# Down-projection operands split in two parts during gate/up, sample rows' product inside gate/up, and another order of the block products

## The chip, the cores and the metric

The kernel runs on one core of one Trainium2 chip. A core has TensorE (PE, with its weight loads listed as PEld), VectorE (DVE), ScalarE (ACT), GpSimd (POOL) and SyncE (SP), which here issues the DMAs. The metric is the device time of one execution in microseconds (us). Shown is the median of three runs.

## The reference, cut to what matters

One decoder layer in float32 for 1024 prompt rows and 64 sample rows (8 sequences of 8), model width 1024. A mixer (attention and a gated unit) comes first; the change lies in the feed-forward part behind it:

```python
D_FF = 2816
def _ffn(h, w_gate, w_up, w_down):
    return (jax.nn.silu(h @ w_gate) * (h @ w_up)) @ w_down
def _post(x, f, gate, g, b):
    return _layer_norm(ALPHA * x + gate * f, g, b)
...
yp = _post(yp, _ffn(_modulate(yp, mp[3], mp[4]), w_gate[l], w_up[l], w_down[l]),
           mp[5], ln2_g[l], ln2_b[l])
```

## The kernel before

**Two parts for each number.** A float32 product is made of three passes in the float32r type: an operand is split in a rounded part hi (a copy on ACT, `split`, L949) and a rest lo = x - hi (a subtraction on DVE, L950), and hi*hi, lo*hi and hi*lo are summed in PSUM (`PASSES`, L955). `load_unit` (L93) loads 512 KB of weights and splits them so.

**Gate/up.** `gate_up` (L860) runs over the 22 units f of 128 rows of D_FF. For each of three column groups c of X (384, 384 and 320 tokens; the last has 256 prompt tokens and the 64 sample tokens) it makes 24 matmuls into a bank of tag "a" for gate and 24 into one of tag "b" for up, then silu on ACT (L872), the multiplication on DVE (L873), and a store into the DRAM tensor `g_d` (L874). Units 0 and 1 run in the order of `CORD` = (2, 0, 1), half of each ahead of the other half, while the last rows of the mixer are still being made (`norm_tile` L818, `to_features` L163: transposes into banks of tag "c"). Units 2 to 21 stand in the loop at L911.

**The down-projection as seven block products.** The product g @ w_down is cut into 2 x 2 blocks (rows of w_down: two halves of 11 units, j = 0 to 10; columns: halves H[0] and H[1]; prompt tokens: two halves). Seven block products replace eight, in the manner of Winograd's form of Strassen's scheme, so sums of blocks are needed. `down_sums` (L899), called in the loop for f = 2 to 12, loads two rows of w_down, makes four sums on DVE and stores them unsplit into `t_d`. Behind gate/up each product runs over j, loads its two operands, adds and splits them on DVE and ACT, and calls `product` (L957): 12 matmuls of 512 columns, three passes for each of four 128-token blocks, into four PSUM banks (`setA`, `setB`). The first loop (L1033) also computes the 64 sample rows (L1054): 88 matmuls with hi and lo of the sample's g side by side as stationary operand, into two banks `sacc`. Then P2 (L1062), P3 (L1079), P4 (L1097), P5 (L1110), P6 (L1121) and the last (L1161). In P6's loop the operands of the last product are prepared, and the last product runs tile by tile.

**The end of a tile.** `residual` (L1017) multiplies by the gate on POOL and adds ALPHA * x1, loaded from `x1_d`. `close_tile` (L1145) takes statistics, multiplies the finished bank by the gate and adds it. `finish` (L984) makes mean and variance, takes the power -0.5 on POOL (L994), normalises on ACT, multiplies by t_lg on POOL (L101), adds t_lb on DVE (L1008) and stores; the very last tile does this on DVE in halves (L996).

**What sets the order.** The kernel is written in program order; the framework (L1290, `schedule_with_timeline_sim=True`) fixes beforehand the order of the instructions of each engine and of the DMA queue on SP, from a simulated time line and with program order as priority, so work is moved forward where its buffers and inputs are free. On the chip each engine follows that order. Buffers come from pools (`raws`/`rw` two each for raw loads, `wts` four and `w2` two for operands); a pool opened where another was closed shares its memory and waits for it.

Of the kernel before, what the change touches and what calls it, by code (L numbers as in the profile page):

```python
# [10 lines left out]
F32 = mybir.dt.float32  # L11
# [32 lines left out]
def tile_block(  # L44
# [23 lines left out]
    t_d = dram.tile([DFF // 2, 4, 512], F32, name="t_d")  # L68
# [685 lines left out]
    with ExitStack() as p3:  # L754
# [104 lines left out]

        def gate_up(f, ws, cs):  # L860
            for c in cs:
                n = CW[c]
# [11 lines left out]
                nc.sync.dma_start(out=g_d[f * P : (f + 1) * P, 384 * c : 384 * c + n], in_=s[:, :n])  # L874
# [8 lines left out]
    with ExitStack() as p4:  # L883
        rw = p4.enter_context(tc.tile_pool(name="rw", bufs=2, side="right", reuse_waits="tile"))
        g1 = p4.enter_context(tc.tile_pool(name="g1", bufs=2 * NJ, side="right", reuse_waits="tile"))
        gp = p4.enter_context(tc.tile_pool(name="gp", bufs=3, side="right", reuse_waits="tile"))
        oa = p4.enter_context(tc.tile_pool(name="oa", bufs=2, side="right", reuse_waits="tile"))
        tl = p4.enter_context(tc.tile_pool(name="tl", bufs=1, side="right", reuse_waits="tile"))
        tp_ctx = ExitStack()
        tp = tp_ctx.enter_context(tc.tile_pool(name="tp", bufs=1, side="right", reuse_waits="tile"))  # L890

        H = (slice(0, 512), slice(512, D))

# [5 lines left out]
        def down_sums(j):  # L899
            r = tp.tile([P, 2, D], F32, tag="r", name="tpr")  # L900
            for u in range(2):
                nc.sync.dma_start(out=r[:, u], in_=w_down[(j + NJ * u) * P : (j + NJ * u + 1) * P, :])
            b11, b12, b21, b22 = r[:, 0, H[0]], r[:, 0, H[1]], r[:, 1, H[0]], r[:, 1, H[1]]
            t = tp.tile([P, 4, 512], F32, tag="t", name="tpt")
            nc.vector.tensor_tensor(out=t[:, 0], in0=b12, in1=b11, op=ALU.subtract)
            nc.vector.tensor_tensor(out=t[:, 2], in0=b22, in1=b12, op=ALU.subtract)
            nc.vector.tensor_tensor(out=t[:, 1], in0=t[:, 2], in1=b11, op=ALU.add)
            nc.vector.tensor_tensor(out=t[:, 3], in0=b21, in1=t[:, 1], op=ALU.subtract)
            nc.sync.dma_start(out=t_d[j * P : (j + 1) * P], in_=t)

        for f in range(2, NF):  # L911
            gate_up(f, gate_up_open(f), range(3))
            if f < 2 + NJ:
                down_sums(f - 2)
            if f == 2 + NJ:
                tp_ctx.close()
                w2 = p4.enter_context(tc.tile_pool(name="w2", bufs=2, side="right", reuse_waits="tile"))
        x_ctx.close()
        g2 = p4.enter_context(tc.tile_pool(name="g2", bufs=2 * NJ, reuse_waits="tile"))
# [28 lines left out]
        def split(w, cols, src):  # L948
            nc.scalar.activation(out=w[:, 0, cols], in_=src, func=AF.Copy)  # L949
            nc.vector.tensor_tensor(out=w[:, 1, cols], in0=src, in1=w[:, 0, cols].bitcast(F32), op=ALU.subtract)  # L950

        def vtt(out, in0, in1, op):
            nc.vector.tensor_tensor(out=out, in0=in0, in1=in1, op=op)  # L953
# [3 lines left out]
        def product(banks, st, mv, first, last, tbs=range(4)):  # L957
            for tb in tbs:
                for q, (sp, wp) in enumerate(PASSES):
                    mm(out=banks[tb], lhsT=st[sp][:, tb * P : (tb + 1) * P], rhs=mv[wp],  # L960
                       start=first and q == 0, stop=last and q == 2, skip_group_check=True)
# [22 lines left out]
        def finish(i, bns, last=False):  # L984
# [3 lines left out]
            bn = bns  # L988
# [7 lines left out]
            if last:  # L996
                for hs in H:
                    nc.vector.scalar_tensor_tensor(  # L998
                        out=yi[:, hs], in0=yi[:, hs], scalar=mv[:rows, 0:1], in1=lg[:, hs], op0=ALU.subtract, op1=ALU.mult
                    )  # L1000
                    nc.vector.scalar_tensor_tensor(  # L1001
                        out=yi[:, hs], in0=yi[:, hs], scalar=rstd[:rows, 0:1], in1=lb[:, hs], op0=ALU.mult, op1=ALU.add
                    )
                    nc.sync.dma_start(out=dst[:, hs], in_=yi[:, hs])
            else:
                normalize_act(yi, yi, mv, rstd, rows)
                pool_tt(yi, yi, lg, ALU.mult)
                vtt(yi, yi, lb, ALU.add)  # L1008
                nc.sync.dma_start(out=dst, in_=yi)

        def stats_half(bn, i, hf):
# [282 lines left out]
```

## Time and profile before

| what | us |
|---|---|
| median of three runs (lowest, highest) | 1244.11 (1240.84, 1245.77) |
| time of the profiled execution | 1243.76 |
| its span, first to last instruction | 1241.9 |
| PE busy in the span | 1174.6 |
| DVE busy | 636.6 |
| ACT busy | 424.9 |
| POOL busy | 230.2 |

The span is what the trace shows; the time has 1.86 us around it. Busy PE includes matmuls whose ends are modelled, so progress is better read from the starts of successive matmuls. In a timeline a row has its start, its length, engine, line, operation and tiles; in brackets stands how long the engine was idle before it and what released it.

### The profile page before, as it was taken

What the parts mean: (1) busy time and instruction counts of PE and PEld (TensorE: products, weight loads), DVE (VectorE), ACT (ScalarE), POOL (GpSimd) and SP (SyncE); (2) the same over time, 40 slices, a digit from 0 to 9 for tenths busy, and PEclk for the clock granted to TensorE, in tenths of its full rate; (3) what the DMA queues carried; (4) which work ended last, traced back from release to release, by engine and by line L of the source; (5) the groups of instructions that cost most, each with busy time, mean ns of one, the idle gap of its engine ahead of it and who ended that gap; (6) DMA issues with size and microseconds to landing.
All of it is one profiled execution on the core that took longest, in us unless ns stands there. A gap on an engine that the chain in (4) does not pass through costs nothing. (4 is left out here: it accounts for less than half of the span.)

```text
span 1241.9 us, 17503 instructions
## 1 busy us (share of the span) xinstructions
PE 1174.6 (95%) x6791; PEld 1043.8 (84%) x6791; DVE 636.6 (51%) x1212; ACT 424.9 (34%) x749; POOL 230.2 (19%) x202
## 2 busy tenths in 40 slices
PE   4999989999889998999999999999999999999992
PEld 2677678887678798999999999999999977888882
DVE  4444355997757975443121112112113359996886
ACT  3563125666742553211111111111112254444612
POOL 2213434554234430000000000000000003012207
PEclk9999999998999998999999999999999999999997
DMA  9844443322363437777122142112113493433643
GB/s 326 273 136 149 133 151 107 94 83 77 102 237 111 155 134 268 271 258 266 61 93 83 68 160 95 62 60 94 59 59 114 160 330 110 128 110 120 208 148 135
DMA packets 82259, 179.74 MB, mean 145 GB/s; under 512 B 12016, under 2 KB 37744, under 8 KB 80752
## 3 DMA queue, kind: packets, MB, share of 16 engines
q1 hardware_dynamic: 82176, 178.62, 42.6%
q8 instruction: 53, 0.87, 0.3%
q14 instruction: 30, 0.25, 0.1%
HBM read 142.02 MB, written 37.55 MB: 145 GB/s over the span
## 5 line engine op out<-in xcount | busy, mean ns | idle before, releaser
L868 PE MATMUL ps_a<-X,unit 128*128 128x384 f32 (+1 forms) x1584 | 278.2, 328 | 0.6 <-DVE unit L97 0.6
L868 PE MATMUL ps_b<-X,unit 128*128 128x384 f32 (+1 forms) x1584 | 276.0, 326 | 0.0
L868 PEld LDWEIGHTS ps_a<-X,unit 128*128 128x128 f32 x1584 | 263.7, 188 | 1.0 <-DVE unit L97 1.0
L868 PEld LDWEIGHTS ps_b<-X,unit 128*128 128x128 f32 x1584 | 263.3, 188 | 0.0
L873 DVE TENSOR_TENSOR s<-ps_b,s 128x384 f32<-128x384 f32 (+1 forms) x66 | 35.2, 534 | 239.0 <-PE ps_b L868 224.5
L872 ACT ACTIVATE s<-ps_a 128x384 f32<-128x384 f32 (+1 forms) x66 | 31.0, 472 | 358.4 <-PE ps_a L868 353.3
L101 POOL TENSOR_TENSOR y<-y,t_gate 128x512 f32<-128x512 f32 x12 | 18.7, 1584 | 613.4 <-ACT y L1057 555.4
L204 PE MATMUL ps_a<-unit,X 128*128 128x512 f32 x456 | 124.7, 412 | 4.5 <-ACT unit L96 2.4
L97 DVE TENSOR_TENSOR unit<-raw,unit 128x1024 fp32r<-128x1024 f32 x63 | 79.1, 1258 | 94.4 <-ACT unit L96 94.4
L204 PEld LDWEIGHTS ps_a<-unit,X 128*128 128x128 f32 x456 | 86.5, 196 | 33.0 <-issue 5.2
L96 ACT ACTIVATE unit<-raw 128x1024 fp32r<-128x1024 f32 x66 | 69.5, 1057 | 79.5 <-issue 39.3
L488 PE MATMUL ps_a<-X,unit 128*128 128x384 f32 (+1 forms) x408 | 78.4, 340 | 6.0 <-ACT z L498 3.3
L953 DVE TENSOR_TENSOR opnd<-rwd,opnd 128x1024 fp32r<-128x1024 f32 x55 | 68.6, 1258 | 20.2 <-ACT opnd L1048 18.4
L488 PEld LDWEIGHTS ps_a<-X,unit 128*128 128x128 f32 x408 | 69.8, 194 | 7.0 <-ACT z L498 3.5
L204 PE MATMUL ps_b<-unit,X 128*128 128x512 f32 x168 | 49.9, 408 | 0.9 <-DVE X L188 0.9
L960 PE MATMUL ps_d<-opnd 128*128 128x512 f32 x198 | 50.5, 391 | 0.1
L960 PE MATMUL ps_c<-opnd 128*128 128x512 f32 x198 | 50.3, 390 | 0.0
L113 POOL TENSOR_TENSOR rstd<-ve,neghalf 128x1 f32<-128x1 f32 (+1 forms) x36 | 29.8, 827 | 109.0 <-DVE ve L111 93.6
L960 PEld LDWEIGHTS ps_d<-opnd 128*128 128x128 f32 x198 | 37.1, 188 | 8.2 <-DVE y L953 0.5
L960 PEld LDWEIGHTS ps_c<-opnd 128*128 128x128 f32 x198 | 37.2, 188 | 8.1 <-DVE y L953 0.2
L172 ACT ACTIVATE h<-ps_c,mod 128x384 f32<-128x384 f32 (+1 forms) x48 | 29.2, 630 | 42.8 <-PE ps_c L169 29.5
L204 PEld LDWEIGHTS ps_b<-unit,X 128*128 128x128 f32 x168 | 32.2, 195 | 9.3 <-DVE X L188 1.3
(279 smaller groups left out, 1668.0 us busy)
## 6 DMA issues: line engine op xcount, KB each, us to landing
rwd<-in_w_down SPq DMA_DIRECT2D x22, 512.0 KB
raw<-in_w_gate SPq DMA_DIRECT2D x22, 512.0 KB
raw<-in_w_up SPq DMA_DIRECT2D x22, 512.0 KB
tpr<-in_w_down SPq DMA_DIRECT2D x22, 512.0 KB
t_d<-tpt SPq DMA_DIRECT2D x11, 1024.0 KB
g<-g_d SPq DMA_DIRECT2D x44, 256.0 KB
rwd<-t_d SPq DMA_DIRECT2D x44, 256.0 KB
g_d<-s SPq DMA_DIRECT2D x44, 192.0 KB
```

Source lines behind the costliest of these rows:

```text
L96: nc.scalar.activation(out=w[:, 0, :], in_=r, func=AF.Copy)
L97: (lo or nc.vector).tensor_tensor(out=w[:, 1, :], in0=r, in1=w[:, 0, :].bitcast(F32), op=ALU.subtract)
L101: nc.gpsimd.tensor_tensor(out=out, in0=in0, in1=in1, op=op)
L113: nc.gpsimd.tensor_tensor(out=rstd[:rows], in0=ve[:rows], in1=neghalf[:rows], op=ALU.pow)
L172: nc.scalar.activation(out=h[:, :npr], in_=pt[:, :npr], func=AF.Identity, scale=scale_of(mod, k)[:, 0:1], bias=shift_of(mod, k)[:, 0:1])
L204: mm(out=pt, lhsT=X[c][:, xp, k, off : off + P], rhs=rhs_of(units, k, wp), start=st and q == 0, stop=sp and q == 2)
L488: mm(out=pt[:, :n], lhsT=w[:, wp, k * P : (k + 1) * P], rhs=X[c][:, xp, k, :], start=(k == 0 and q == 0), stop=(k == KD - 1 and q == 2))
L868: mm(out=pt[:, :n], lhsT=w[:, wp, k * P : (k + 1) * P], rhs=X[c][:, xp, k, :], start=(k == 0 and q == 0), stop=(k == KD - 1 and q == 2))
L872: nc.scalar.activation(out=s[:, :n], in_=pp[0][:, :n], func=AF.Silu)
L873: nc.vector.tensor_tensor(out=s[:, :n], in0=pp[1][:, :n], in1=s[:, :n], op=ALU.mult)
L953: nc.vector.tensor_tensor(out=out, in0=in0, in1=in1, op=op)
L960: mm(out=banks[tb], lhsT=st[sp][:, tb * P : (tb + 1) * P], rhs=mv[wp], start=first and q == 0, stop=last and q == 2, skip_group_check=True)
```

## The change

Gate/up, besides its old work, now makes the operands of the down-projection in two parts, and the sample rows' product:

- `gate_up` stores only the prompt columns of g. The 64 sample columns are split at once into `gs` and kept in the dictionary `GS`.
- `down_row(f)` replaces `down_sums`. For every unit f it loads row f of w_down, splits it on ACT and DVE and makes the four matmuls of the sample rows into `sacc` (tags "c" and "d"). For f of 11 and more (j = f - 11) it also stores the split half H[1] of that row, loads row j, makes the four sums, stores the first unsplit into `t1_d`, splits the other three and stores both parts of each into `t_d`, which now has room for four operands in two parts. Its pool `tp` lies on the left side and is closed behind gate/up.
- Units 2 to 21 run in the order of `CORD`.
- Four of the products (third, fifth, sixth, seventh) load their moving operand in two parts straight into the operand buffer (`moving`), without ACT or DVE; the first, second and fourth load it unsplit and split it (`moving_split`).
- The order becomes: A11 B11; A12 B21 (last before), in banks of its own; then the third to seventh as below. The last product is the one with A22, and it runs tile by tile over its accumulating banks.
- The gate multiplication of `residual`, the normalisation and the multiplication by t_lg move from POOL and ACT to DVE in all tiles; statistics are taken as halves are finished (`add_and_stats`). Tiles 0 to 3 are finished ahead of the last product, tiles 4 to 7 behind it.

```diff
-                nc.sync.dma_start(out=g_d[f * P : (f + 1) * P, 384 * c : 384 * c + n], in_=s[:, :n])
+                nc.sync.dma_start(out=g_d[f * P : (f + 1) * P, 384 * c : 384 * c + npr], in_=s[:, :npr])
+                if n > npr:
+                    gs = f0.tile([P, 2, NS], F32R, tag="gs", name=f"gs{f}", bufs=3)
+                    nc.scalar.activation(out=gs[:, 0], in_=s[:, npr:n], func=AF.Copy)
+                    nc.vector.tensor_tensor(
+                        out=gs[:, 1], in0=s[:, npr:n], in1=gs[:, 0].bitcast(F32), op=ALU.subtract
+                    )
+                    GS[f] = gs
...
+        sacc = [bank("c"), bank("d")]
+
+        def row_split(src):
+            o = tp.tile([P, 2, D], F32R, tag="o", name="tpo", bufs=2)
+            nc.scalar.activation(out=o[:, 0], in_=src, func=AF.Copy)
+            vtt(o[:, 1], src, o[:, 0].bitcast(F32), ALU.subtract)
+            return o
+
+        def down_row(f):
+            j = f - NJ
+            r = tp.tile([P, D], F32, tag="r", name="tpr", bufs=2)
+            nc.sync.dma_start(out=r, in_=w_down[f * P : (f + 1) * P, :])
+            o = row_split(r)
+            for hf in range(2):
+                for wp in range(2):
+                    mm(out=sacc[hf], lhsT=GS[f].rearrange("p a b -> p (a b)"), rhs=o[:, wp, H[hf]],
+                       start=f == 0 and wp == 0, stop=f == NF - 1 and wp == 1)
+            if j < 0:
+                return
+            rows = slice(j * P, (j + 1) * P)
+            nc.sync.dma_start(out=t_d[rows, 0], in_=o[:, :, H[1]].bitcast(F32))
+            r0 = tp.tile([P, D], F32, tag="r", name="tpr0", bufs=2)
+            nc.sync.dma_start(out=r0, in_=w_down[rows, :])
+            t = tp.tile([P, 4, 512], F32, tag="t", name="tpt")
+            vtt(t[:, 0], r0[:, H[1]], r0[:, H[0]], ALU.subtract)
+            vtt(t[:, 2], r[:, H[1]], r0[:, H[1]], ALU.subtract)
+            vtt(t[:, 1], t[:, 2], r0[:, H[0]], ALU.add)
+            vtt(t[:, 3], r[:, H[0]], t[:, 1], ALU.subtract)
+            nc.sync.dma_start(out=t1_d[rows, :], in_=t[:, 0])
+            o = row_split(t[:, 1:3].rearrange("p a b -> p (a b)"))
             for u in range(2):
...
+                nc.sync.dma_start(out=t_d[rows, 1 + u], in_=o[:, :, H[u]].bitcast(F32))
+            o = tp.tile([P, 2, D], F32R, tag="o", name="tpo", bufs=2)
+            nc.scalar.activation(out=o[:, 0, H[0]], in_=t[:, 3], func=AF.Copy)
+            vtt(o[:, 1, H[0]], t[:, 3], o[:, 0, H[0]].bitcast(F32), ALU.subtract)
+            nc.sync.dma_start(out=t_d[rows, 3], in_=o[:, :, H[0]].bitcast(F32))
 
         for f in range(2, NF):
-            gate_up(f, gate_up_open(f), range(3))
-            if f < 2 + NJ:
-                down_sums(f - 2)
...
+            gate_up(f, gate_up_open(f), CORD)
+            if f == 2:
+                down_row(0)
+                down_row(1)
+            down_row(f)
+        tp_ctx.close()
+        w2 = right("w2", 2)
...
+        def moving(src):
+            w = operand()
+            nc.sync.dma_start(out=w[:, :, H[1]].bitcast(F32), in_=src)
+            return w
+
+        def moving_split(src):
+            w = operand()
+            r = raw()
+            nc.sync.dma_start(out=r[:, 0:512], in_=src)
+            split(w, H[1], r[:, 0:512])
+            return w
...
+        setA = [bank(t) for t in "abcd"]
...
+            A11.append(g_half(g1, j, 0))
+            w = moving_split(w_down[j * P : (j + 1) * P, H[0]])
+            split(w, H[0], A11[j])
+            product(setA, *pair(w), j == 0, j == NJ - 1)
...
+        setB = [bank(t) for t in "abcd"]
         for j in range(NJ):
...
+            w = moving_split(t1_d[j * P : (j + 1) * P, :])
+            t = oa.tile([P, 512], F32, tag="ot", name="ot")
+            nc.sync.dma_start(out=t, in_=g_d[j * P : (j + 1) * P, 512:1024])
+            vtt(t, t, A22[j], ALU.add)
+            split(w, H[0], t)
+            product(setB, *pair(w), j == 0, j == NJ - 1)
+        for tb in range(4):
+            add_and_stats(tb, 0)
+        for tb in range(4):
+            nc.scalar.activation(out=y[:, 4 + tb, H[1]], in_=setB[tb], func=AF.Copy)
...
         for j in range(NJ):
-            w = operand()
-            r = t_half(j, 2)
+            w = moving(t_part(j, 2))
             split(w, H[0], A21[j])
-            split(w, H[1], r[:, H[1]])
             product(setA, *pair(w), False, j == NJ - 1)
+            o = [g1.tile([P, 512], F32R, tag="g", name="ah")]
+            o += [g2.tile([P, 512], F32R, tag="g", name=n_) for n_ in ("al", "bh", "bl")]
+            nc.scalar.activation(out=o[0], in_=A22[j], func=AF.Copy)
+            vtt(o[1], A22[j], o[0].bitcast(F32), ALU.subtract)
+            for lo in range(2):
+                nc.sync.dma_start(out=o[2 + lo].bitcast(F32), in_=t_part(j, 3)[:, lo])
+            ops.append(o)
+        for tb in range(4):
+            add_and_stats(tb, 1)
+            finish(tb, bns[tb])
...
         for tb in range(4):
             vtt(y[:, 4 + tb, H[1]], setA[tb], y[:, 4 + tb, H[1]], ALU.add)
...
         for tb in range(4):
-            close_tile(4 + tb, setA[tb])
...
+            i = 4 + tb
             for j in range(NJ):
                 ah, al, bh, bl = ops[j]
                 for q, (sp, wp) in enumerate(PASSES):
...
+                    mm(out=setA[tb], lhsT=(ah, al)[sp][:, tb * P : (tb + 1) * P], rhs=(bh, bl)[wp],
+                       start=False, stop=j == NJ - 1 and q == 2, skip_group_check=True)
+        for tb in range(4):
+            add_and_stats(4 + tb, 1)
+        for tb in range(4):
+            i = 4 + tb
+            t = oa.tile([P, 512], F32, tag="ot", name="ot")
+            vtt(t, setA[tb], tails["gate"][:, H[0]], ALU.mult)
+            nc.vector.scalar_tensor_tensor(
+                out=y[:, i, H[0]], in0=y[:, i, H[0]], scalar=ALPHA, in1=t, op0=ALU.mult, op1=ALU.add
+            )
+            stats_half(bns[i], i, 0)
+            finish(i, bns[i], tb == 3)
```

More of the change, by code (lines that the diff above doesn't have):

```diff
@@ L1011, in stats_half @@
-        def stats_half(bn, i, hf):
-            rows = rows_of(i)
-            nc.vector.bn_stats(out=bn[:rows, hf, :], in_=y[:rows, i, H[hf]])
-        x1t = {}
-        def residual(i, hf, acc=None):
-            rows = rows_of(i)
-            if i not in x1t:
-                x1t[i] = raw()
-                nc.sync.dma_start(out=x1t[i][:rows], in_=x1_d[i * P : i * P + rows, :])
+            for hs in H if last else (slice(0, D),):
+                nc.vector.scalar_tensor_tensor(
+                    out=yi[:, hs], in0=yi[:, hs], scalar=mv[:rows, 0:1], in1=lg[:, hs], op0=ALU.subtract, op1=ALU.mult
+                )
+                nc.vector.scalar_tensor_tensor(
+                    out=yi[:, hs], in0=yi[:, hs], scalar=rstd[:rows, 0:1], in1=lb[:, hs], op0=ALU.mult, op1=ALU.add
+                )
+                nc.sync.dma_start(out=dst[:, hs], in_=yi[:, hs])
@@ L1075, in tile_block @@
         for tb in range(4):
+            nc.scalar.activation(out=y[:, tb, H[0]], in_=setA[tb], func=AF.Copy)
+        setC = [bank(t) for t in "abcd"]
+        for j in range(NJ):
+            A12.append(g_half(g2, j + NJ, 0))
+            w = moving_split(w_down[(j + NJ) * P : (j + NJ + 1) * P, H[0]])
+            split(w, H[0], A12[j])
+            product(setC, *pair(w), j == 0, j == NJ - 1)
+        for hf in range(2):
+            add_and_stats(8, hf)
+        finish(8, bns[8])
+        for tb in range(4):
+            vtt(y[:, tb, H[0]], setC[tb], y[:, tb, H[0]], ALU.add)
@@ L1079, in tile_block @@
         for j in range(NJ):
-            w = operand()
-            t = t_half(j, 1)
-            vtt(A21[j], A11[j], A21[j], ALU.subtract)
-            vtt(t[:, H[0]], A22[j], A21[j], ALU.subtract)
-            nc.scalar.activation(out=w[:, 0, :], in_=t, func=AF.Copy)
-            vtt(w[:, 1, :], t, w[:, 0, :].bitcast(F32), ALU.subtract)
-            product(setA, *pair(w), False, j == NJ - 1)
-        for hf in range(2):
-            residual(8, hf)
-        bn8 = small.tile([P, 2, 6], F32, tag="bn", name="bn8")
@@ L1105, in tile_block @@
+            t = oa.tile([P, 512], F32, tag="ot", name="ot")
+            vtt(t, A12[j], A22[j], ALU.subtract)
+            vtt(t, t, A21[j], ALU.add)
+            split(w, H[0], t)
             product(setB, *pair(w), False, j == NJ - 1)
@@ L1159, in tile_block @@
         for tb in range(4):
-            close_tile(4 + tb, setA[tb])
-        for tb in range(4):
-            acc = bank("aabb"[tb])
+            i = 4 + tb
             for j in range(NJ):
```

197 lines of the change are left out of this document (52 added, 145 removed).

## The prediction

> **What bounds the kernel now.** I read the page first, then busy time by stretch, then TensorE's (PE's) rows in order of time, then the end. P1 to P7 are the seven block products in program order.
>
> ```profile
> span 1241.9 us, 17503 instructions
> PE 1174.6 (95%) x6791; PEld 1043.8 (84%) x6791; DVE 636.6 (51%) x1212; ACT 424.9 (34%) x749; POOL 230.2 (19%) x202
> ```
>
> ```profile
> 447.70:585.00 137.30, 132.77 (x800) 131.41 (x798) 73.93 (x121) 41.16 (x65) 11.33 (x9) 0.98 0.72 254
> 585.00:700.00 115.00, 115.00 (x702) 115.00 (x701) 20.28 (x25) 16.64 (x24) 0.00 (x0) 1.00 0.27 91
> ...
> 980.00:1035.00 55.00, 53.12 (x234) 42.86 (x232) 34.41 (x44) 28.30 (x41) 2.96 (x3) 1.00 0.82 286
> 1035.00:1066.00 31.00, 30.05 (x123) 24.06 (x124) 30.85 (x35) 14.66 (x15) 6.92 (x4) 0.94 0.36 109
> ...
> 1220.00:1242.00 22.00, 0.00 (x0) 0.00 (x0) 15.94 (x23) 3.72 (x3) 13.23 (x7) 0.61 0.36 143
> ```
>
> The columns are the stretch, its length, busy time of PE, PEld, DVE, ACT and POOL, granted clock, DMA share and GB/s. Gate/up has PE full (115.00 of 115.00) with DVE and ACT four fifths idle. The products are nearly full too, and the last 22 us have no matmul at all.
>
> ```profile
> 531.53 4.35 PE L868 MATMUL ps_a<-X,unit 128*128 128x384 f32 x24
> ...
> 555.23 4.35 PE L868 MATMUL ps_a<-X,unit 128*128 128x384 f32 x24
> ```
>
> ```profile
> 981.83 1.55 PE L960 MATMUL ps_c<-opnd,oa 128*128 128x512 f32 x6
> ...
> 1035.53 0.73 PE L960 MATMUL ps_a<-opnd 128*128 128x512 f32 x2 [2.12 <-ACT opnd L1068]
> ...
> 1036.92 1.84 PE L960 MATMUL ps_a<-opnd 128*128 128x512 f32 x4 [0.20 <-DVE opnd L953]
> ...
> 1172.95 1.53 PE L960 MATMUL ps_c<-opnd 128*128 128x512 f32 x6
> ...
> 1175.68 1.52 PE L960 MATMUL ps_c<-opnd 128*128 128x512 f32 x6
> ...
> 1204.16 15.57 PE L1166 MATMUL ps_b<-o,o 128*128 128x512 f32 x66
> ```
>
> One unit f of gate/up takes 555.23 - 531.53 = 23.70 us for 144 matmuls, without gaps. Twelve 512-column matmuls, one step j of a product, take 1175.68 - 1172.95 = 2.73 us: 0.2275 us each. From 981.83 to the end of the last matmul (1204.16 + 15.57 = 1219.73) are 237.9 us for 7 x 132 + 88 = 1012 matmuls, which need 230.2. So only **7.7 us** of that stage is lost, most of it at 1033 to 1040: a gap of 2.12 us, then four matmuls in 1.84 us instead of 0.91. [...]
>
> **The end.** Rows in order of time:
>
> ```profile
> 1220.55 0.68 DVE L953 TENSOR_TENSOR tt<-ps_b,t_gate 128x512 f32<-128x512 f32 x1
> ...
> 1227.02 5.29 POOL L101 TENSOR_TENSOR y<-y,t_lg 128x1024 f32<-128x1024 f32 x2
> ...
> 1230.05 3.35 DVE L953 TENSOR_TENSOR y<-y,t_lb 128x1024 f32<-128x1024 f32 x1 [1.52 <-POOL y L101]
> 1233.31 0.68 DVE L953 TENSOR_TENSOR y<-y,tt 128x512 f32<-128x512 f32 x1
> 1234.03 0.69 DVE L1013 BATCH_NORM_STATS2 bn<-y 128x6 f32<-128x512 f32 x1
> 1234.63 1.21 DVE L953 TENSOR_TENSOR y<-y,t_lb 128x1024 f32<-128x1024 f32 x1
> ...
> 1238.16 0.99 SPq L1004 DMA_DIRECT2D out<-y  x2
> ```
>
> The last tile is not slow by its own work: its 'y<-y,tt' at 1233.31 stands in DVE's queue behind two 't_lb' additions, which wait for POOL's multiplications by t_lg; one takes 3.35 us beside POOL, the next 1.21.
>
> **The change, part by part.** Base: this execution, span 1241.9, time 1243.76 (1.86 us around the span), 0.35 us under the median 1244.11.
>
> *Sample rows' product into gate/up.*
>
> ```profile
> L1054 PE MATMUL ps_a<-opnd,gs 128*128 128x512 f32 x44 | 15.1, 394 | 0.0
> L905 DVE TENSOR_TENSOR tpt<-tpr 128x512 f32<-128x512 f32 x11 | 7.5, 686 | 36.5 <-DMA tpr<-in_w_down 36.5
> L97 DVE TENSOR_TENSOR unit<-raw,unit 128x1024 fp32r<-128x1024 f32 x63 | 79.1, 1258 | 94.4 <-ACT unit L96 94.4
> L96 ACT ACTIVATE unit<-raw 128x1024 fp32r<-128x1024 f32 x66 | 69.5, 1057 | 79.5 <-issue 39.3 <-DMA raw<-in_w_u 14.3 <-DMA raw<-in_w_o 5.5
> ```
>
> 2 x 44 matmuls, 20.0 us, go from one stage where PE is full to another: -20.0 + 20.0 = **0**. They use banks c and d, which gate/up leaves idle, and stand in program order after unit f, when their operands have had most of 23.7 us.
>
> *Operands made in gate/up.* From f = 11 on a unit adds to DVE four 512-column operations (4 x 0.69), two 1024-column lower parts (2 x 1.26), a short one (0.69) and a tiny one: 6.0 us; to ACT 2 x 1.06 + 0.6 = 2.7 us; to SP 7 more DMAs. DVE has 20.28 of 115 us busy there, so 4.2 + 6.0 of 23.7: hidden, cost **0**. If that cover were gone, PE would wait for row f's operand (a rival below).
>
> *Start of gate/up.*
>
> ```profile
> 474.85 0.90 SPq L902 DMA_DIRECT2D tpr<-in_w_down  x2
> 475.86 0.39 SPq L831 DMA_DIRECT2D x_d<-r  x1
> ...
> 483.20 1.24 ACT L126 ACTIVATE r<-r,nb,rstd 128x1024 f32<-128x1024 f32 x1 [4.65 <-DMA x_d<-r]
> ...
> 484.50 0.69 PE L169 MATMUL ps_c<-ident,r 128*128 128x128 f32 x2 [3.34 <-ACT r L126]
> ```
>
> ```profile
> 478.00:484.00 6.00, 3.16 (x19) 2.84 (x17) 3.00 (x5) 1.29 (x2) 0.00 (x0) 1.00 0.99 333
> 484.00:490.00 6.00, 4.95 (x18) 4.50 (x19) 2.15 (x5) 4.55 (x9) 0.00 (x0) 0.52 1.01 406
> 514.00:520.00 6.00, 6.00 (x37) 6.00 (x36) 2.62 (x3) 1.11 (x2) 0.00 (x0) 1.00 1.01 413
> ```
>
> down_sums runs ahead of its place, and its loads (two rows at 474.85) are queued ahead of the store of x1 (475.86). ACT may overwrite r only when that store has landed, at 483.2, 7 us after its issue with the DMA engines full. PE is idle 3.34 us, then has a clock of 0.52 over 4.95 busy us (2.4 us lost): 5.7 us. The new down_row holds its operand until unit f is through, so after rows 0 and 1 it can't run ahead, and its stores begin at f = 11. What may be late next are the loads of the tail constants, which stay, and to_features, which shares bank tag c with the new accumulator. Bounds: -6.5 (with the short gaps beside it) and +2 (one more gap like that of 1035.53); I take **-5**, nearer the first, as the transfers named by the waiting row go.
>
> *P1 to P7.* Per step j DVE does 2, 2, 3, 3, 3, 2, 0 operations of 512 columns, 165 in all.
>
> ```profile
> 1199.00 0.68 DVE L1153 SCALAR_TENSOR_TENSOR y<-y,tt 128x512 f32<-128x512 f32 x1
> 1199.60 0.68 DVE L953 TENSOR_TENSOR tt<-ps_d,t_gate 128x512 f32<-128x512 f32 x1
> ...
> L825 DVE SCALAR_TENSOR_TENSOR r<-r,mv,lg 128x1024 f32<-128x1024 f32 x8 | 10.2, 1272 | 0.0
> L101 POOL TENSOR_TENSOR y<-y,t_lg 128x1024 f32<-128x1024 f32 x7 | 19.7, 2825 | 0.6 <-ACT y L126 0.6
> 980.00:1242.00 262.00, 236.79 (x1026) 192.42 (x1024) 209.35 (x286) 113.51 (x155) 53.71 (x31) 0.96 0.50 169
> ```
>
> They follow each other at 0.60 to 0.69 us, say 0.64: 106 us. About 70 more for residuals, statistics and additions make 45, nine normalisations at 2 x 1.27 + 0.35 make 26: 177 against 209.35 before, though POOL's work moved to DVE. The waits on POOL's multiplications (2825 ns each) go, but for that on the power of the variance. The wait of 1035.53 goes too: all splits of P1 are 512 columns, and the sample sums stand beside P2, not ahead of its first operand. New on the path: P5 accumulates on the banks of P4, so its first matmul waits for ACT's copy; the first bank is done nine matmuls (2.05 us) early, so 0 to 1 us. P7 starts on the banks of P6 and waits for DVE's addition, ahead of which stand in program order tile 0 to 3's residual, statistics and normalisation: 4 x (3 x 0.64 + 2.9) = 19 us. P6 gives DVE 22 x 0.64 + 19 + 5 = 38 us of work for 30 us of PE; six operand buffers of lead and a lighter P5 take up part. Bounds: 0, and 11 us (four normalisations ahead) with 2.4 us of slow clock; I take 3.5, near the measured gap of 2.12 with its slow matmuls. With 1 us for P4 to P5 and 0.8 for P7's single-bank order (15.57 us for 66, 0.006 each above 0.2275) 5.3 us are lost instead of 7.7: **-2.4**.
>
> On such a gap, the Trainium skill (TensorE: Matmul & The Clock Gate, Why this matters for your kernels) asks only that no idle gap exceeds about 3 us. Row 1036.92 disagrees: 2.12 us of idleness already halved the rate; by the page the sum would be 1 us lower.
>
> *The end.* The last tile does one multiplication (0.68), one addition (0.72 to the next), then what row 1234.03 and its successors take, 1241.9 - 1234.03 = 7.87, less 1.2 for the foreign 't_lb': with some 0.15 to start 0.15 + 0.68 + 0.72 + 6.67 = 8.2 us behind the last matmul instead of 22.2. Tiles 4 to 6 need some 5 us of DVE each while PE gives 7.5, so DVE should be free; 1.0 us for a remainder: **-13.0**. Bounds -14 and, if DVE enters P7 with 11 us of work, -8.
>
> Sum: 0 + 0 - 5 - 2.4 - 13.0 = -20.4; 1243.76 - 20.4 = **1223**.
>
> **Rivals.**
> *Only the end gains.* The gap at 484 comes back through the tail constants' loads, and the gaps at new bank changes eat what the old ones cost: 1243.76 - 13 = 1231. For it: 53.12 of 55.00 and 30.05 of 31.00 show how little the products can give.
> *DVE is late at P7.* 13 us there and a tail of 14 instead of 9, the start as forecast: 1223 + 10 + 5 = 1238. For it: the 38 us above; against it, 32 us less DVE work and no stretched rows like 1230.05.
> *Transfers are late in P6.* P6 asks for 11.5 MB of operands (11 x 1.05), plus 1.05 of x1: 12.6 MB in 30 us is 418 GB/s, and the fullest window moved 413. Six operands can come in P5, outputs can go later; if they don't, at 349 GB/s (286 / 0.82) it takes 36 us: +6, slow clock +2.4: 1231. The Trainium skill (DMA: Bandwidth & Descriptors, Where 436 GB/s comes from) puts the limit from HBM at about 358 GB/s per core, which would give this rival 35 us; the window with 413 GB/s speaks against so low a limit.
> *Slower.* The row operands of gate/up come late. Two buffers serve three operands per unit: from f = 11 split (2.4), sums (2.7), split (2.4), store, split (1.3), store.
>
> ```profile
> 447.31 0.80 SPq L902 DMA_DIRECT2D tpr<-in_w_down  x2
> ...
> 452.19 0.68 DVE L905 TENSOR_TENSOR tpt<-tpr 128x512 f32<-128x512 f32 x1
> ```
>
> With some 5 us for each transfer (447.31 to 452.19) that is a cycle of 19 to 20 us against 23.70 + 0.91. It decides from about 26.4 us on, as a unit's lead (20 us over 11 units) then runs out; at 30 us 11 x 5.4 - 20 = 39 us of waits: 1262.
>
> **How the numbers follow.** Forecast 1223 (1213 to 1228): 46%. Only the end: 20%. DVE late, 1238: 15%. Transfers late: 8%. Slower: 9%. Better than 1213: 2%. A measurement of this kernel tells 0.5% (6.2 us) from no change: under 1237.9 lie the first two, the transfers and about half of DVE's case, 83%; 8% lie within, 9% above. The range 1213 to 1238 leaves out the slower case, half of DVE's and the best.
>
> **What would show it.** Right: no PE gap at 480 to 490; units of 23.70 + 0.91 us; P1 to P7 in about 216 us; 8 to 10 us from the last matmul to the end; POOL with power operations only. Wrong: PE gaps before the sample rows' matmuls in gate/up, a gap at P6 to P7 over 5 us, or DVE without idle time through P7.

## The result and the profile after

The kernel after takes **1213.51 us** (median of four runs, 1213.11 to 1216.29) against 1243.47 for the kernel before (four runs, 1240.84 to 1245.77): a ratio of 0.9765 (95% interval 0.974 to 0.9789), 30 us less. The forecast was 1223, with a range of 1213 to 1238: the measured time lies 9.5 us under the forecast and only 0.5 us above the lower end of the range. The profiled execution took 1213.78 us. Its page begins with:

```profile
span 1212.0 us, 17677 instructions
...
PE 1167.8 (96%) x6791; PEld 1040.2 (86%) x6791; DVE 642.6 (53%) x1255; ACT 421.0 (35%) x774; POOL 189.3 (16%) x180
```

PE has the same 6791 matmuls, and its idle time has gone from 1241.9 - 1174.6 = 67.3 us to 44.2, most of the 29.9 us. Busy time by stretch, columns as in the prediction:

```profile
440.00:506.46 66.46, 66.46 (x414) 64.86 (x413) 41.21 (x71) 35.26 (x55) 13.46 (x9) 1.00 0.35 118
506.46:991.00 484.54, 484.54 (x2910) 481.27 (x2909) 155.63 (x209) 108.79 (x164) 0.00 (x0) 1.00 0.44 154
...
1025.00:1055.00 30.00, 30.00 (x133) 24.66 (x132) 25.20 (x41) 13.52 (x24) 1.46 (x1) 1.00 0.83 276
...
1145.00:1172.75 27.75, 27.75 (x123) 22.87 (x122) 23.42 (x39) 3.16 (x5) 6.83 (x4) 1.00 0.79 280
1172.75:1203.60 30.85, 30.81 (x132) 24.45 (x131) 22.51 (x35) 0.00 (x0) 4.36 (x3) 1.00 0.13 51
1203.60:1212.00 8.40, 0.00 (x0) 0.00 (x0) 5.09 (x9) 0.00 (x0) 0.92 (x1) 0.71 0.17 64
```

From 440 us to the last matmul PE is never idle and never below full clock, where before it was busy 4.95 of 6 us at a clock of 0.52 (484 to 490). What is left behind the last matmul is 8.4 us. PE's rows in order of time give the borders of the stages:

```profile
445.11 3.62 PE L871 MATMUL ps_a<-X,unit 128*128 128x320 f32 x23
...
506.30 4.35 PE L871 MATMUL ps_a<-X,unit 128*128 128x384 f32 x24
...
522.97 0.62 PE L928 MATMUL ps_c<-tpo,gs 128*128 128x512 f32 x2
...
530.92 4.35 PE L871 MATMUL ps_a<-X,unit 128*128 128x384 f32 x24
...
991.79 0.85 PE L997 MATMUL ps_a<-opnd 128*128 128x512 f32 x3
...
1171.90 0.85 PE L997 MATMUL ps_d<-opnd 128*128 128x512 f32 x3
1172.59 0.40 PE L1158 MATMUL ps_a<-bh,ah 128*128 128x512 f32 x1
...
1203.16 0.40 PE L1158 MATMUL ps_d<-bl,ah 128*128 128x512 f32 x1
```

A unit takes 530.92 - 506.30 = 24.62 us (forecast: 23.70 + 0.91). Gate/up begins at 445.11, the products at 991.79, the last matmul ends at 1203.56. Read in the same way, all kernels of this study divide as follows (profiled executions, in us; "sample" is where the 88 matmuls of the sample rows are made):

| kernel | start | gate/up | products | behind the last matmul | sample |
|---|---|---|---|---|---|
| before | 447.7 | 534.1 | 237.9 | 22.2 | products |
| after | 445.1 | 546.7 | 211.8 | 8.4 | gate/up |
| one sample unit | 444.8 | 542.0 | 211.9 | 8.7 | 4 matmuls |
| one sample unit, rows held | 445.7 | 527.2 | 211.8 | 8.4 | 4 matmuls |
| unsplit operands | 443.9 | 546.7 | 211.8 | 8.2 | gate/up |
| POOL closes tiles | 449.4 | 546.7 | 212.4 | 10.0 | gate/up |
| tiles 0 to 3 close late | 444.5 | 546.7 | 211.8 | 14.9 | gate/up |
| last product in pairs | 447.3 | 546.7 | 211.8 | 13.0 | gate/up |
| before, DVE closes tiles | 445.0 | 532.5 | 238.5 | 19.4 | products |
| before, rows held | 446.8 | 526.2 | 237.7 | 22.8 | products |
| before, late gates | 443.3 | 534.2 | 233.1 | 22.9 | products |
| before, all three | 444.5 | 526.2 | 235.5 | 18.3 | products |

The start lies anywhere between 443.3 and 449.4, in the mixer, whose code the change does not touch; its mean is 445.5 over the five kernels with the old order of the products and 445.8 over the seven with the new one, so the 2.6 us between before and after are taken as scatter between executions. The sample rows' 88 matmuls are counted at 0.2275 us each, 20.0 us. The rest of the 29.9 us is gate/up, 534.1 + 20.0 - 546.7 = **7.5**, the products, 237.9 - 20.0 - 211.8 = **6.1**, and the end, 22.2 - 8.4 = **13.7**.

The end, on DVE:

```profile
1162.74 3.67 DVE L1040 SCALAR_TENSOR_TENSOR y<-y,rstd,t_lb 128x1024 f32<-128x1024 f32 x3
1170.74 0.69 DVE L903 TENSOR_TENSOR y<-ps_a,y 128x512 f32<-128x512 f32 x1 [4.33 <-PE ps_a L997]
...
1203.60 0.69 DVE L903 TENSOR_TENSOR ot<-ps_d,t_gate 128x512 f32<-128x512 f32 x1 [2.21 <-PE ps_d L1158]
1204.33 0.69 DVE L1166 SCALAR_TENSOR_TENSOR y<-y,ot 128x512 f32<-128x512 f32 x1
1205.05 0.69 DVE L1023 BATCH_NORM_STATS2 bn<-y 128x6 f32<-128x512 f32 x1
...
1206.09 1.41 DVE L1037 SCALAR_TENSOR_TENSOR y<-y,mv,t_lg 128x512 f32<-128x512 f32 x2
1207.41 1.41 DVE L1040 SCALAR_TENSOR_TENSOR y<-y,rstd,t_lb 128x512 f32<-128x512 f32 x2
```

DVE has finished tiles 0 to 3 at 1166.4, before the last product begins, and waits 2.21 us for the last bank. Behind it stand the last tile's own operations only, to 1208.8; the remaining 3.2 us are its store.

### The profile page after: what moved, and what is told of

Read it like the earlier page. It is cut to its first block, busy times and chain, and to the rows that moved or that the text cites. A ratio compares the mean times of both kernels' runs of the same rounds, so it can differ in the third digit from the quotient of the medians.

```text
span 1212.0 us, 17677 instructions
## 1 busy us (share of the span) xinstructions
PE 1167.8 (96%) x6791; PEld 1040.2 (86%) x6791; DVE 642.6 (53%) x1255; ACT 421.0 (35%) x774; POOL 189.3 (16%) x180
## 4 chain that ended last, share of the span: by engine, by line
PE 87%; DVE 8%; ACT 1%; issue 1%; DMA 1%; POOL 1%; SPq 1%; DVEq 0%; ACTq 0%; POOLq 0%
PE ps_a L871 22%; PE ps_b L871 22%; PE ps_a L205 9%; PE ps_a L997 4%; PE ps_c L997 4%; PE ps_b L997 4%; PE ps_d L997 4%; PE ps_b L205 3%; PE ps_d L205 2%; PE ps_a L489 2%; PE ps_c L170 1%; PE ps_d L357 1%; DVE s L607 1%; DVE bn L108 1%; DVE s L589 1%
## 5 line engine op out<-in xcount | busy, mean ns | idle before, releaser
L1034 POOL TENSOR_TENSOR rstd<-ve,neghalf 128x1 f32<-128x1 f32 (+1 forms) x9 | 13.6, 1511 | 721.5 <-DVE ve L1032 721.5
L997 PE MATMUL ps_c<-opnd 128*128 128x512 f32 x198 | 56.0, 391 | 0.0
L997 PE MATMUL ps_a<-opnd 128*128 128x512 f32 x198 | 55.8, 391 | 0.0
L997 PE MATMUL ps_b<-opnd 128*128 128x512 f32 x198 | 55.7, 390 | 0.0
L997 PE MATMUL ps_d<-opnd 128*128 128x512 f32 x198 | 55.7, 389 | 0.0
L114 POOL TENSOR_TENSOR rstd<-ve,neghalf 128x1 f32<-128x1 f32 (+1 forms) x36 | 29.5, 821 | 107.1 <-DVE ve L112 91.5
L997 PEld LDWEIGHTS ps_b<-opnd 128*128 128x128 f32 x198 | 37.2, 188 | 8.4
```

Of the source, the lines that this page charges most:

```text
L114: nc.gpsimd.tensor_tensor(out=rstd[:rows], in0=ve[:rows], in1=neghalf[:rows], op=ALU.pow)
L1034: nc.gpsimd.tensor_tensor(out=rstd[:rows], in0=ve[:rows], in1=neghalf[:rows], op=ALU.pow)
```

## The experiments

Three questions: is the sample rows' product really free in gate/up, and what do the split operands bring (first two runs and the held one); why is the end short; what made the gaps of before. Each ratio is to the kernel before, run on the same chip as the experiment. The kernel after was measured in the first series only, and the median of the kernel before lay between 1240.64 and 1243.47 us in the four series; so a difference in time to the kernel after is uncertain by up to 3 us, and the stretches in the table above are the firmer measure.

### One unit of the sample rows' product

```diff
-                for wp in range(2):
+                for wp in range(2) if f == NF - 1 else ():
                     mm(out=sacc[hf], lhsT=GS[f].rearrange("p a b -> p (a b)"), rhs=o[:, wp, H[hf]],
-                       start=f == 0 and wp == 0, stop=f == NF - 1 and wp == 1)
+                       start=wp == 0, stop=wp == 1)
```

> The changed kernel with the sample rows' matmuls left out for 21 of 22 units (84 of 88; the sample rows of the output are those of one unit alone). Theory: PE has no gap from gate/up to the last matmul, so the moved product costs its full price in its new place: 84 x 0.2275 = 19.1 us less than the changed kernel, about 1194 us. Rival: in gate/up it fills time in which PE would have waited; then at most 10 us less, 1203 us or more.

Measured: 1211.94 us (1209.22 to 1213.77), a ratio to before of 0.9748 (0.9724 to 0.9772). Taking away 19.1 us of matmuls brought 1.6 (4.7 in gate/up of the profiled execution, 546.7 to 542.0). The time fits the rival (1203 us or more), but not its reason: PE does not wait in gate/up of the kernel after, the waits are new. PE's rows in order of time show where they went:

```profile
483.03 0.59 PE L170 MATMUL ps_c<-ident,r 128*128 128x128 f32 x2 [3.24 <-ACT r L127]
486.12 1.54 PE L170 MATMUL ps_c<-ident,r 128*128 128x128 f32 x6 [2.50 <-ACT h L173]
...
509.98 0.53 PE L871 MATMUL ps_b<-X,unit 128*128 128x320 f32 x2 [2.19 <-DVE s L876]
511.02 5.47 PE L871 MATMUL ps_a<-X,unit 128*128 128x320 f32 x26 [0.51 <-DVE unit L98]
```

The gap of before is back, at the same instruction (transposes waiting for r, 3.24 us; before 3.34 at 484.50). SP's queue in this run, then in the kernel after, and the DMA share by stretch, this run first:

```profile
474.10 0.33 SPq L924 DMA_DIRECT2D tpr<-in_w_down  x1
475.30 0.45 SPq L832 DMA_DIRECT2D x_d<-r  x1
477.36 3.62 SPq L924 DMA_DIRECT2D tpr<-in_w_down  x2
```

```profile
461.34 7.99 SPq L832 DMA_DIRECT2D x_d<-r  x2
```

```profile
506.00:600.00 94.00, 90.87 (x543) 90.06 (x542) 56.11 (x75) 32.97 (x46) 0.00 (x0) 0.98 0.94 342
```

```profile
506.00:600.00 94.00, 94.00 (x564) 93.31 (x563) 22.30 (x29) 18.55 (x28) 0.00 (x0) 1.00 0.30 107
```

Loads of rows of w_down (L924) stand between the stores of x1 (L832) again, where the kernel after has its last two stores of x1 one behind the other and no such load until 501.35. From 506 to 600 the DMA engines are busy 0.94 of the time, against 0.30 in the kernel after. With no matmul reading the row operands, their two buffers come free as soon as the row is split and stored, and the rows run ahead by many units: the last of their loads is issued at 616.22, when gate/up has 370 us to go. So this run did not take away one thing but two: the matmuls and the brake.

### The same with the rows held back

```diff
-            gate_up(f, gate_up_open(f), CORD)
-            if f == 2:
-                down_row(0)
-                down_row(1)
-            down_row(f)
+            stores = gate_up(f, gate_up_open(f), CORD)
+            with tc.issue_after(stores[0].ins):
+                if f == 2:
+                    down_row(0)
+                    down_row(1)
+                down_row(f)
```

(`gate_up` returns its stores to `g_d`; the four matmuls left are those of the run above.)

> The kernel after, again with 84 of the 88 matmuls of the sample rows left out (only the last unit's four are made, so the sample output is not the full sum), and each unit's DMAs of the row operands (loads and stores) queued on SP behind the first g_d store of their own unit. Theory: the sample rows' product costs its 20 us of TensorE wherever it stands, and the run without it lost them again because nothing held the row transfers back (waits of 3.2, 2.5 and 2.2 us in gate/up, DMA share 0.94 from 506 to 600 us where the kernel after has 0.30). Held back, gate/up has no gap of over 1 us, takes 526.7 + 0.9 us, and the time is 1213.5 - 19.1 = 1194, within 1191 to 1198. Rival: the matmuls of the sample rows filled time in which TensorE would have waited anyway; then gaps come at other places and the time stays above 1205.

Measured: 1194.87 us (1193.92 to 1196.07), ratio 0.9628 (0.9611 to 0.9644), as the theory said; the rival falls.

```profile
506.00:600.00 94.00, 94.00 (x573) 94.00 (x573) 24.89 (x31) 20.67 (x30) 0.00 (x0) 1.00 0.37 123
```

PE is full, the DMA share is 0.37. Gate/up takes 527.2 us, 19.5 less than in the kernel after and 14.8 less than in the run above; by their number the 84 matmuls cost 84 x 0.2275 = 19.1 us. The same run shows that the rows running ahead were the cause of the gaps in the run above. Whether they hurt by their place in SP's queue or by filling the DMA engines isn't told apart.

### Operands stored unsplit

```diff
-            o = row_split(t[:, 1:3].rearrange("p a b -> p (a b)"))
-            for u in range(2):
-                nc.sync.dma_start(out=t_d[rows, 1 + u], in_=o[:, :, H[u]].bitcast(F32))
...
+            nc.sync.dma_start(out=t_d[rows], in_=t[:, 1:4])
...
-            w = moving(t_part(j, 1))
+            w = moving_split(t_part(j, 0))
```

(and so for the three other products that load such parts; sums still made in gate/up.)

> The changed kernel with the sums of w_down's blocks stored unsplit and split on ACT and DVE in the third, fifth, sixth and last product, as before the change. Theory: DVE gets 44 more operations of 512 columns behind gate/up (28 us), 22 of them in the sixth product, where its queue is fullest, so PE waits at the last product: 4 to 12 us more than the changed kernel, 1218 to 1226 us. Rival: DVE still has room and PE covers it: within 2 us of the changed kernel.

Measured: 1213.28 us (1212.37 to 1214.69), ratio 0.9761 (0.974 to 0.9782): the same as after, as the rival said; the theory falls. Busy time from 1085 to 1170 us, this kernel first, then the kernel after:

```profile
1085.00:1170.00 85.00, 85.00 (x374) 69.88 (x373) 81.04 (x136) 38.97 (x68) 2.71 (x2) 1.00 0.51 156
```

```profile
1085.00:1170.00 85.00, 85.00 (x374) 69.88 (x373) 68.87 (x111) 21.97 (x36) 6.83 (x4) 1.00 0.84 285
```

Splitting inside the products raises DVE from 68.87 to 81.04 of 85.00 us and ACT from 21.97 to 38.97, and lowers the DMA share from 0.84 to 0.51. PE is full in both. Making the operands in two parts ahead of time gives nothing that can be measured here, though it leaves DVE more room.

### Who closes the tiles: ACT and POOL in the kernel after

```diff
+            if not last:
+                normalize_act(yi, yi, mv, rstd, rows)
+                pool_tt(yi, yi, lg, ALU.mult)
+                vtt(yi, yi, lb, ALU.add)
+                nc.sync.dma_start(out=dst, in_=yi)
+                return
...
-            vtt(yi, yi, gt, ALU.mult)
+            pool_tt(yi, yi, gt, ALU.mult)
```

> The changed kernel with the normalisation of all tiles but the last on ACT and POOL, and the gate multiplication of the residuals on POOL, as before the change. Theory A: POOL's work in the path of DVE's queue made the long end: 6 to 13 us more than the changed kernel, 1219 to 1226 us. Theory B: eight tiles closed in the last 30 us made it, and the new order, which closes four of them ahead of the last product, cures it by itself: 0 to 3 us more, 1213 to 1217 us.

Measured: 1218.13 us (1215.49 to 1220.32), ratio 0.9792 (0.9766 to 0.9818): 4.6 us more than after, between the two theories. Its profiled execution is 6.5 us longer than that of the kernel after: 4.3 by a late start (449.4), 0.6 in the products and 1.6 at the end. Without the late start, which other kernels have without this edit, 2.2 us remain, within theory B's 0 to 3:

```profile
1208.51 0.69 DVE L903 TENSOR_TENSOR ot<-ps_d,t_gate 128x512 f32<-128x512 f32 x1 [3.17 <-PE ps_d L1164]
...
1209.84 1.22 DVE L903 TENSOR_TENSOR y<-y,t_lb 128x1024 f32<-128x1024 f32 x1
```

One addition of t_lb for another tile still stands in the last tile's way, but DVE had waited 3.17 us for the last bank: with four tiles left, POOL's slow multiplications find time.

### Who closes the tiles: DVE in the kernel before

```diff
-                normalize_act(yi, yi, mv, rstd, rows)
-                pool_tt(yi, yi, lg, ALU.mult)
-                vtt(yi, yi, lb, ALU.add)
-                nc.sync.dma_start(out=dst, in_=yi)
+            for hs in H if last else (slice(0, D),):
+                nc.vector.scalar_tensor_tensor(
...
-            pool_tt(yi, yi, gt, ALU.mult)
+            vtt(yi, yi, gt, ALU.mult)
```

> The kernel before with the normalisation of all tiles and the gate multiplication of the residuals on DVE, as after the change; order of the products unchanged. Theory A (POOL's work): 8 to 13 us less than before, 1231 to 1236 us. Theory B (eight tiles at the end): DVE alone then has some 43 us of work from 1196 on and ends at about 1239: 2 to 4 us less than before, 1240 to 1242 us.

Measured: 1239.56 us (1237.17 to 1243.47), ratio 0.9974 (0.9961 to 0.9987): 2.9 us less than before. The last matmul ends at 1216.03, and DVE goes on:

```profile
1217.60 0.68 DVE L953 TENSOR_TENSOR tt<-ps_b,t_gate 128x512 f32<-128x512 f32 x1
...
1222.52 0.67 DVE L953 TENSOR_TENSOR tt<-ps_b,t_gate 128x512 f32<-128x512 f32 x1
...
1225.04 1.27 DVE L1000 SCALAR_TENSOR_TENSOR y<-y,rstd,t_lb 128x1024 f32<-128x1024 f32 x1
...
1230.90 1.41 DVE L1000 SCALAR_TENSOR_TENSOR y<-y,rstd,t_lb 128x512 f32<-128x512 f32 x2
```

No row from 1202 us on has an idle time before it. The last tile's gate multiplication starts at 1222.52, 6.5 us behind its last matmul, though no wait on POOL's multiplications is left: the queue is full with other tiles' work. So waiting for POOL was not the main reason for the long end. The run puts POOL's work on DVE, though, so it does not tell what the waits alone cost.

### Tiles 0 to 3 closed late in the kernel after

```diff
-        for tb in range(4):
-            add_and_stats(tb, 1)
-            finish(tb, bns[tb])
...
-            vtt(y[:, 4 + tb, H[1]], setA[tb], y[:, 4 + tb, H[1]], ALU.add)
+            mark = nc.vector.tensor_tensor(
+                out=y[:, 4 + tb, H[1]], in0=setA[tb], in1=y[:, 4 + tb, H[1]], op=ALU.add
+            )
+        with tc.issue_after(mark.ins):
+            for tb in range(4):
+                add_and_stats(tb, 1)
+                finish(tb, bns[tb])
```

> The kernel after, with the second half and the normalisation of tiles 0 to 3 queued on DVE behind the last addition at the start of the last product, so that eight tiles close during and behind the last product, as in the kernel before. Theory (the place of the first four tiles makes the end short): DVE has 24.45 us of work in the last product and 6.2 behind it, and gets 4 x 4.6 = 18.5 us more, 49 us from 1172.8 on: the end of the span moves from 1212 to about 1222, the last matmul stays at 1203.6, time 1223 (1219 to 1226), with DVE busy without a gap behind 1173. Rival (DVE's own normalisation and multiplication make the end short, wherever the tiles close): the four tiles fit into the 6.4 us that DVE is idle and the time is 1216 or less.

Measured: 1220.4 us (1219.32 to 1222.44), ratio 0.9838 (0.9816 to 0.9859), 6.9 us more than after and as the theory said; the rival falls. All that changed is the time behind the last matmul, 14.9 instead of 8.4 us:

```profile
1170.14 0.69 DVE L1147 TENSOR_TENSOR y<-ps_a,y 128x512 f32<-128x512 f32 x1 [13.03 <-PE ps_a L997]
...
1203.23 0.66 DVE L903 TENSOR_TENSOR ot<-ps_d,t_gate 128x512 f32<-128x512 f32 x1
1203.82 1.26 DVE L1040 SCALAR_TENSOR_TENSOR y<-y,rstd,t_lb 128x1024 f32<-128x1024 f32 x1
...
1213.31 1.40 DVE L1040 SCALAR_TENSOR_TENSOR y<-y,rstd,t_lb 128x512 f32<-128x512 f32 x2
```

DVE is idle 13 us ahead of the last product, where it had closed tiles 0 to 3 in the kernel after, and then has no gap until 1214.7. Its work from 1173 on is 42 us, less than the 49 expected. The 49 took DVE's work in the last product to be 24.45 us, which is the column of the weight loads; DVE's is 22.51, and it idles 8.3 us there. Part of the rest is that operations of different tiles follow each other at 0.60 us, those of one tile at 0.73.

### The gaps of before: block sums held, and gate loads late

First the loads and stores of the block sums, queued behind the first store of their own unit:

```diff
-            gate_up(f, gate_up_open(f), range(3))
+            stores = gate_up(f, gate_up_open(f), range(3))
...
-                down_sums(f - 2)
+                with tc.issue_after(stores[0].ins):
+                    down_sums(f - 2)
```

> The kernel before with the loads of each call of the block sums issued behind the first store of its own unit of gate/up, so that they can't run ahead. Theory: the PE gap at 481 to 485 us and the slow clock behind it come from those transfers, queued ahead of the store of x1: both go, 5 to 8 us less than before, 1236 to 1239 us. Rival: the loads of the tail constants or the next wait in line keep the gap: within 2 us of before.

Measured: 1234.96 us (1233.34 to 1235.42), ratio 0.9938 (0.9926 to 0.995), 7.4 us less than before.

```profile
470.00:500.00 30.00, 30.00 (x184) 29.85 (x183) 8.78 (x18) 12.63 (x22) 0.55 (x1) 1.00 0.33 97
```

PE is full at full clock where before had its gap. Gate/up takes 526.2 us instead of 534.1, 7.9 less: as much as the change gains in gate/up (7.5), from one edge in a queue.

Then the sixteen small loads of the sample rows' gates, behind the second product's loads:

```diff
-                for bb in range(8):
-                    nc.sync.dma_start(
-                        out=gs_[8 * bb : 8 * bb + 8, H[hf]], in_=gate_d[j + 1 + bb : j + 2 + bb, :].to_broadcast([8, 512])
-                    )
...
             product(setB, *pair(w), j == 0, j == NJ - 1)
+        sample_gates()
```

> The kernel before with the 16 small loads of the sample rows' gates behind the loads of the second product instead of ahead of them. Theory: the PE gap at 1033 to 1036 us came from the second product's first operands standing behind those loads and behind the sample sums on ACT and DVE; without it and its slow clock 4 to 6 us less than before, 1238 to 1240 us. Rival: the operands are late anyway (DVE is busy throughout that stage): within 2 us of before.

Measured: 1236.41 us (1235.3 to 1240.32), ratio 0.9959 (0.9945 to 0.9973), 6.0 us less than before. SP's queue and ACT in the kernel before, then SP, ACT and PE in this run:

```profile
1022.97 6.76 SPq L977 DMA_DIRECT2D rwd<-gate_d  x16
...
1029.82 12.44 SPq L941 DMA_DIRECT2D rwd<-t_d  x6
...
1033.45 0.59 ACT L1073 ACTIVATE y<-ps_a 64x512 f32<-64x512 f32 x1
...
1034.43 2.95 ACT L1068 ACTIVATE opnd<-rwd 128x1024 fp32r<-128x1024 f32 x3
```

```profile
1018.60 23.73 SPq L941 DMA_DIRECT2D rwd<-t_d  x11
...
1022.71 1.04 ACT L1073 ACTIVATE opnd<-rwd 128x1024 fp32r<-128x1024 f32 x1
...
1033.90 2.58 PE L960 MATMUL ps_a<-opnd 128*128 128x512 f32 x10 [0.27 <-DVE y L953]
```

Sixteen loads of 8 x 512 numbers (16 KB) each kept the queue for 6.76 us, and the second product's operands could only be issued at 1029.82, 5.7 us before PE began on them at 1035.53. On ACT their first split (1034.43) then stands behind the copies of the sample sums (from 1033.45), which wait for the last sample matmul. With the small loads moved, the order fixed beforehand puts three of those splits ahead of the copies, the first at 1022.71. So the run removes the late issue and the place of the sample sums together, as its expectation says; which of the two ended the wait in the kernel before is not told apart. The wait of 2.12 us and the slow matmuls behind it go, and the products take 4.8 us less. In the kernel after these loads stand earlier:

```profile
1000.04 8.24 SPq L1014 DMA_DIRECT2D rwd<-gate_d  x16
```

They are through at 1008.3, 13.5 us ahead of the second product (991.79 + 132 x 0.2275 = 1021.8), and PE has no gap there.

### The three edits of before together

DVE closes the tiles, block sums held, gate loads late, as above:

```diff
-                normalize_act(yi, yi, mv, rstd, rows)
...
+                with tc.issue_after(stores[0].ins):
+                    down_sums(f - 2)
...
+        sample_gates()
```

> The kernel before with all three at once: normalisation on DVE, block sums held to their units, sample gates loaded later; no operand in two parts, no sample product in gate/up, old product order. Theory: the three parts add up, 5 to 8 + 4 to 6 + the result of the first alone; what is then missing to the changed kernel (some 8 to 16 us, 1222 to 1232 us) is due to the order of the products, which closes four tiles early. Rival: these three are all there is: 1213 to 1217 us.

Measured: 1227.92 us (1226.24 to 1230.49), ratio 0.9891 (0.9875 to 0.9906), 14.4 us less than before, nearly the sum of the three (16.3). To the kernel after 14.4 are still missing; by the table 9.8 of its profile's difference lie behind the last matmul (18.3 against 8.4) and 3.7 in the products (235.5 - 20.0 against 211.8). The products take 2.4 us more than with the late gate loads alone, because PE waits for DVE there, 0.47 us at 1025.98 and then

```profile
1029.58 2.57 PE L965 MATMUL ps_a<-opnd 128*128 128x512 f32 x10 [1.95 <-DVE y L958]
```

So not all that is missing is due to the order in which tiles are closed.

### The last product in pairs of banks

```diff
-        for tb in range(4):
-            i = 4 + tb
-            for j in range(NJ):
+        for t0 in (0, 2):
+            for j, tb in ((j, tb) for j in range(NJ) for tb in (t0, t0 + 1)):
```

> The kernel after, with the last product run in two pairs of banks (a and b alternating every three matmuls, then c and d) instead of bank by bank. Theory (33 matmuls in a row into one bank are slower, 0.2333 us each against 0.2275 where the bank changes every three): the 132 matmuls take 30.0 us instead of 30.8. Rival (the operands of this product, which lie in other buffers, make the difference): they stay at 30.8. By both, two tiles close together at the end: from the last matmul to the end of the span about 12.5 us instead of 8.4, time 1216 to 1218.

Measured in one execution: 1220.44 us, with gate/up starting 2.2 us later than in the kernel after. The product's first and last matmuls:

```profile
1174.73 0.40 PE L1157 MATMUL ps_a<-bh,ah 128*128 128x512 f32 x1
...
1205.30 0.40 PE L1157 MATMUL ps_d<-bl,ah 128*128 128x512 f32 x1
```

1205.70 - 1174.73 = 30.97 us, exactly as in the kernel after (1172.59 to 1203.56): the theory of the banks is wrong. Behind the last matmul it takes 13.0 us, as two tiles close at once: by this one execution closing tile by tile is worth 4.6 us. The time lies above the 1216 to 1218 expected, most of it by the late start.

## Why the prediction was right, and where not

The parts of the sum and their direction were right, but each part that gained was put too small: by 2.5 us at the start of gate/up, 3.7 in the products and 0.7 at the end. With the 2.6 us of scatter in the start that is the distance from the forecast to the profiled time. That the time still lies inside the range, by 0.5 us, is in part luck.

**Sample rows' product, 0: right.** The 84 matmuls taken away cost 19.1 us in gate/up by their number; in the run with the rows held gate/up was 19.5 us shorter than in the kernel after and the time 18.6 us (1213.51 - 1194.87). So they cost in gate/up about what the sum takes off the products (20.0 for 88), and PE never waits for them.

**Operands made in gate/up, 0: right**, shown from the other side too: leaving the split in the products costs nothing (1213.28), as DVE at 81.04 of 85.00 us still keeps up.

**Start of gate/up, -5: right in kind, too small.** It was 7.5, 1 us beyond the lower bound of -6.5. The term priced one wait and the slow matmuls behind it (5.7 us) from two windows. Nearly all the time by which gate/up of before exceeded the 526.2 us that it takes without gaps went, the short gaps too. The reason given, that the row's operand is held until its unit is through, is shown by the two runs on it: without the matmuls that hold it the gap of 3.24 us came back, and with an edge in SP's queue in their place it went again. Held rows alone, in the kernel before, gain as much (7.9), so neither the sample rows' product nor the new order of the column groups was needed for it.

**P1 to P7, -2.4: too small; it was -6.1.** Of the 7.7 us lost before, 1.6 are left (211.8 - 924 x 0.2275), where the sum left 5.3. Three things were in that sum.
- The wait at 1035.53 goes: right. The reasons given were narrower splits and the place of the sample sums. The place of the sample sums is borne out by ACT's rows, but what put them there was, by the run with the late gate loads, the sixteen small issues in SP's queue, worth 4.8 us in the products. The prediction had read DVE and ACT at that place, but not SP. The other 1.3 us were not tried.
- The new waits at the start of P5 and P7 (1 + 3.5 us): wrong. The step that failed is "ahead of which stand in program order tile 0 to 3's residual, statistics and normalisation". Program order is only the priority, as the description of the kernel itself says; the order fixed beforehand puts each operation where its inputs are ready, and by the row at 1162.74 all four normalisations were through at 1166.4, 4.33 us before DVE could do anything for P7. P7's first matmul follows P6's last without a gap (1171.90, 1172.59). DVE was not late but idle there. The estimate of 38 us of DVE work for P6 counted work that was moved ahead: eight of the eleven lower parts for P7 (al<-g,ah) and four of P6's own were made before 1140.62, and from there to 1166.4 DVE was busy for 25.8 us. For P5 too PE has no gap.
- The 0.8 us for the order of P7: size right ((1203.16 - 1172.59) / 131 = 0.2334 us from start to start, 0.8 us over 132 matmuls), reason wrong, as the run in pairs shows.

**The end, -13.0: size right (-13.7), reason only in part.** The prediction put the long end to POOL's multiplications in DVE's queue. Taking these away in the kernel before saved 2.8 us behind the last matmul, and putting them back in the kernel after cost 1.6. Closing tiles 0 to 3 behind the last addition of P6 cost 6.5. So the order of the products, which leaves four tiles instead of eight for the last 30 us, is the larger of the parts that were tried. The 8.4 us that remain are the last tile's own operations and store, as worked out from before's rows (8.2). The parts come from different kernels; added up, they leave about 13.7 - 6.5 - 2.8 = 4.4 us of the end whose cause stays open.

**The rivals.** None came. Gate/up and the products both gained, so it was not the end only; DVE was not late at P7. Transfers in P6 were not late: from 1145 to 1172.75 they moved 280 GB/s with PE full. Row operands in gate/up were not late: a unit kept to 24.62 us. On the length of a harmless gap, the Trainium skill (TensorE: Matmul & The Clock Gate, Why this matters for your kernels) asks that none exceeds about 3 us. The first experiment agrees with the prediction's row against it: behind 2.19 us at 509.98, and 0.51 more at 511.02, 26 matmuls of 320 columns took 5.47 us, where 23 take 3.62 in the row at 445.11. But the length of a gap alone does not decide it here: in the kernel before the granted clock was 0.66 from 350 to 355 us, around a gap of 2.00 us at 351.18, and 1.00 from 195.5 to 205 us, behind a gap of 2.77 us at 195.55; and in the run with the three edits ten matmuls went at their full rate behind 1.95 us (2.57 us, row 1029.58).

## What to carry to other kernels

Read SP's queue at every gap of PE: two of the three gains here, the second for the most part, could be had in the kernel before by moving DMA issues alone, and a small load takes as much of that queue as a big one. Matmuls that hold a buffer also hold back the transfers that would fill it again, so before taking work away ask what it was keeping in place. At the end, count how many results are still to be closed when the last product begins, and order the products so that few are, before making the closing itself faster.

## What was not expected of the hardware

- A small DMA took SP as long as a large one: sixteen of 16 KB kept the queue 6.76 us, 0.42 us each (8.24 us in the kernel after), while an issue of a whole row of w_down took 0.33.
- The matmuls of the last product follow each other at 0.2334 us, those of the six products ahead of it at (1172.59 - 991.79) / 792 = 0.2283, with 512 columns in both. It isn't the order of the banks. The operands lie in other buffers there; whether that is the reason wasn't tried.
- The same operations on DVE follow each other at 0.60 us where they are independent and at 0.73 where each needs the one before (1203.60, 1204.33, 1205.05): a tile closed alone takes a fifth longer than in a mixed queue.
